# A residual block on one core: squares moved from GpSimd to ScalarE, two more plain input tiles, another first pair, a later forget gate

## The chip, the cores and the metric

The kernel runs on one core of a Trainium2 chip. The metric is the device time of one execution in microseconds (us), here the median of three runs. TensorE multiplies matrices, VectorE and ScalarE do elementwise work, GpSimd a little of it and some transfers, and SyncE's queue issues the other transfers.

## What is computed

One layer of a residual block on 528 tokens (16 learned ones and 512 of the input) of 2048 channels, in float32:

```python
h  = rmsnorm(r, mix_pre_g)
z  = h @ w_in + b_in          # q | k | v | forget logits | pool input | gates
logf = log_sigmoid(f_logit)   # 8 heads; its running sum over tokens biases the attention
attn = forgetting_attention(q, k, v, logf)
m  = sigmoid(g_attn) * (attn @ w_attn_o) + sigmoid(g_pool) * (pool(u) @ w_pool_o)
r  = r + rmsnorm(m @ w_out, mix_post_g)
r  = r + rmsnorm(conv_ffn(rmsnorm(r, ffn_pre_g)), ffn_post_g)
```

The change lies in the first part, `h @ w_in`, where q, k, v, the gates and the forget logits are made.

## The kernel before, in words

Channels lie on partitions, tokens along the row, so x is 16 tiles of 128 x 528 (`xr[k]`). A float32 product is made of three reduced ones: each operand is split into a high part, a ScalarE copy, and a low part, a VectorE subtraction; high times high, high times low and low times high are added up in a PSUM bank. For weights that is `make_hi` and `make_lo` (L193 and L201, tiles `whi` and `wlo`), for x `split_x` (L369 and L370, tiles `xb`, or `xh` and `xl` from k = 8 on), for token sums `split_sums` (L520 and L524, tiles `ht` and `lt`). The weights of 128 output channels, a tile, come in two halves of 1024 columns, each a "unit" with a high and a low part; six raw halves, four high and four low ones have a place.

The loop over k streams x. For every k it splits x, squares it (L396, L400, L402: ScalarE for even k and for 0 and 1, GpSimd for odd k) and adds the square up (`square_sum`, L382: even k on VectorE into one accumulator, odd k on GpSimd into another), and TensorE does 4 products for the forget logits (bank pair `pf`, L407) and 6 for the first tile of q (`pq`, L375). A product takes 264 columns, half of the tokens.

After that, tiles are made in one of two ways. A **plain tile** (`x_step`, banks `pk`) takes 16 x 6 = 96 products. A **pair** of tiles (`strassen`) takes 7 x 24 = 168 products, for two tiles, by a Strassen scheme with seven block products: its seven weight blocks are called 11, 12, S2, S1, S3, S4 and 22 (S1 to S4 are sums of blocks, made on VectorE, `wsum`), and they meet the blocks 11, 21, T2, T1, T3, 22 and T4 of x. T1 to T4 are the token sums: differences of token halves of x, made in place in `xr` by `sums_of_x` (L538 scales on ScalarE, L543 subtracts on VectorE), then split into `ht` and `lt`. Before, four tiles are plain (`NC = 4`) and the rest of q, k and v goes in ten pairs, then pool inputs and gates in further pairs.

The order of the work on each engine is the order in which the program records it. Two lanes of side work (`Side`) give out a piece at each step of TensorE's loops; a `yield` says how many microseconds of products should pass before the next piece. `norm_x` makes `rstd`, the factor of the norm, by a product with ones (`ps_rs`) and a reciprocal; `x_evac` (L589) multiplies the finished banks of a plain tile by `rstd` on VectorE, and `x_out` adds the bias on ScalarE (L578) and stores from GpSimd's queue. `logits` (L430, L431) empties `pf` after the second plain tile. `forget` computes log-sigmoid on 8 rows, by halves of 264 columns, and its running sum in ten doubling steps on VectorE (L435 to L459); it starts in the second lane with the first pair. In a pair, ScalarE's copy of bank `pua` (L491) has to be done before the third block product, which adds onto that bank.

Of the kernel before, what the change touches and what calls it, by code (L numbers as in the profile page):

```python
# [35 lines left out]
P = 128  # L36
# [38 lines left out]
def block(ctx, tc, xT, win, wf, wao, wpw, wpo, wout, wup, wdn, consts, out):  # L75
# [22 lines left out]

    order = []

    NC = 4
    qkv = [t for h in range(H) for t in (h, 8 + h, 16 + h)]
    xpairs = list(zip(qkv[NC::2], qkv[NC + 1::2]))
    gates = [(32 + i, 33 + i) for i in range(0, 32, 2)]
# [19 lines left out]
    }  # L124


    loads, units, base = [], [], []
    for key in order:
        base.append(len(units))
        if key[0] == "pair":  # L130
            at0 = len(loads)
            for src in key[1:]:
                loads += [(srcs[src[0]](src[1]), c) for c in (0, 1024)]
            units += [(i, at0) for i in ("11", "12", "S2", "S1", "S3", "S4", "22")]
        else:
# [32 lines left out]
    def make_source():  # L168
        i = at["sum"]
        kind, n = units[i]  # L170
        if kind == "":
            sources[i] = raw_of(n)
        else:
            a11, a12, a21, a22 = (raw_of(n + j) for j in range(4))
            if kind == "S2":
                for name in ("S1", "S2"):
                    sums[name] = wp.tile([P, 1024], F32, name="wsum", tag="wsum", bufs=2)
                dve.tensor_tensor(sums["S1"], a21, a22, op=OP.add)
                dve.tensor_tensor(sums["S2"], sums["S1"], a11, op=OP.subtract)  # L179
            elif kind == "S3":  # L180
                dve.tensor_tensor(a21, a11, a21, op=OP.subtract)
                drop(n)
            elif kind == "S4":
                dve.tensor_tensor(a12, a12, sums["S2"], op=OP.subtract)  # L184
            sources[i] = {"11": a11, "12": a12, "S3": a21, "S4": a12, "22": a22}.get(kind) or sums[kind]
        at["sum"] += 1

    def make_hi():
# [185 lines left out]
            for e in range(2):  # L374
                pe.matmul(pss[e], w[a], xb[e, k][b], start=k == 0 and j == 0, stop=k == KT - 1 and j == 2)  # L375

    xacc = [F("acc"), F("acc")]
    sq = {}

    def square_sum(k):  # L380
        if k >= 2:
            (pool if k % 2 else dve).tensor_tensor(xacc[k % 2], xacc[k % 2], sq.pop(k), op=OP.add)  # L382

    pf, pq = ([s_ps(n)[:, :XN] for _ in range(2)] for n in ("pf", "pq"))
    w_f = lambda k: wf_s2[k // 8][:, k % 8]
# [1 line left out]
    for k in range(KT):  # L387
        g = wfr[:, KT * H + k:KT * H + k + 1]
        if k == 0:
            split_f(0)  # L390
        split_x(k, g)
        if k == 1:
            w_q = weights("in", 0, ahead=0)
            split_f(1)
        if k < 2:
            act.activation(xacc[k], xr[k], AF.Square)  # L396
        else:
            sq[k] = F("sq")
            if k % 2:
                pool.tensor_tensor(sq[k], xr[k], xr[k], op=OP.mult)  # L400
            else:
                act.activation(sq[k], xr[k], AF.Square)  # L402
        if k >= 3:
            square_sum(k - 3)
        for j in range(2):
            for e in range(2):
                pe.matmul(pf[e], w_f(k), xb[e, k][j], start=k == 0 and j == 0, stop=k == KT - 1 and j == 1)  # L407
        for kk in ((), (0, 1))[k == 1] if k < 2 else (k,):
            x_step(pq, w_q(kk), kk)
        if k == 7:  # L410
            make_lo()
    for k in range(KT - 3, KT):
        square_sum(k)
    rstd = cp.tile([P, L], F32, name="rstd")
    c_dram = dp.tile([H, L], F32, name="c_dram")
# [2 lines left out]
    cmeta = cp.tile([2, H, META], F32, name="cmeta")  # L418

    def norm_x():  # L420
        dve.tensor_tensor(xacc[0], xacc[0], xacc[1], op=OP.add)
        yield 8.0
        rstd_from(xacc[:1], rstd, L)

    fx = F("fx")[:H]

# [6 lines left out]
    def forget():  # L433

        dve.tensor_tensor(fx, fx, rstd[:H], op=OP.mult)  # L435
        yield 2.0
        act.activation(fx, fx, AF.Identity, bias=cs[:H, C_BF:C_BF + 1])
        yield 2.0
        ab, ln = F("fab")[:H], F("fln")[:H]
        fa, fb = ab[:, :XN], ab[:, XN:]  # L440
        for e in range(2):
            x, fc = fx[:, XN * e:XN * (e + 1)], ln[:, XN * e:XN * (e + 1)]
            act.activation(fa, x, AF.Abs)
            act.activation(fa, fa, AF.Exp, scale=-1.0)
            yield 2.0
            dve.tensor_scalar(fb, fa, 1.0, None, op0=OP.add)
            yield 2.0
            act.activation(fc, fb, AF.Ln)
            yield 2.0
            dve.tensor_scalar(fb, fb, -1.0, None, op0=OP.add)  # L450
            dve.tensor_tensor(fa, fa, fb, op=OP.subtract)
            dve.tensor_tensor(fc, fc, fa, op=OP.add)
            dve.scalar_tensor_tensor(x, x, 0.0, fc, op0=OP.min, op1=OP.subtract)
            yield 2.0
        cur, nxt = fx, ab
        sh = 1
        while sh < L:
            dve.tensor_copy(nxt[:, :sh], cur[:, :sh])
            dve.tensor_tensor(nxt[:, sh:], cur[:, sh:], cur[:, :L - sh], op=OP.add)  # L459
            cur, nxt = nxt, (ln if nxt is ab else ab)  # L460
            sh *= 2
            yield 3.0
        nc.gpsimd.dma_start(c_dram, cur)
        nc.gpsimd.dma_start(cmeta, c_dram[:, :META].unsqueeze(0).to_broadcast([2, H, META]))
        yield 1.0
# [13 lines left out]
    def strassen(keys, blocks, n, skip=0, late=None):  # L479
# [26 lines left out]
        dve.tensor_tensor(gr, gr, c[:, skip:], op=OP.add)  # L506
        return zg, zv


    xts = {}  # L510
    qkv_dram = dp.tile([24, P, L], F32, name="qkv_dram")
# [20 lines left out]

    def sums_of_x():

        for k in range(HK + 1):
            if k < HK:
                for i in (k, HK + k):
                    act.activation(xr[i], xr[i], AF.Identity, scale=wfr[:, KT * H + i:KT * H + i + 1])  # L538
            yield 1.2
            if k < HK:  # L540
                (b11, b12), (b21, b22) = ((xr[i][:, :XN], xr[i][:, XN:]) for i in (k, HK + k))
                for dst, a, b in ((b11, b12, b11), (b12, b22, b12), (b22, b22, b11), (b21, b21, b22)):
                    dve.tensor_tensor(dst, a, b, op=OP.subtract)  # L543
            if 1 <= k <= KX:
                yield from split_sums(xts, x_tiles(k - 1), XN)
# [55 lines left out]
    XBLOCKS.update({n: lambda k, n=n: xts[n, k] for n in ("T1", "T2", "T3", "T4")})  # L601
    side.add(norm_x())
    side2.add(sums_of_x())
    for m in qkv[1:NC]:
        w = weights("in", m)
        pss = [s_ps("pk")[:, :XN] for _ in range(2)]
        for k in range(KT):
            x_step(pss, w(k), k)
            for lane in (side, side2):
                lane.tick(6 * XN / 2330.0)  # L610
        if m == qkv[1]:
            side.finish()
            logits()
            x_evac(qkv[0], pq)
        x_evac(m, pss)
    side2.finish()
    side2.add(split_sums(xts, [t for k in range(KX, HK) for t in x_tiles(k)], XN))
    side2.finish()
    side2.add(forget())
    for ma, mb in xpairs:  # L620
        last = (ma, mb) == xpairs[-1]
        za, zb = strassen((("in", ma), ("in", mb)), XBLOCKS, XN, late=d_loads() if last else None)
        side.add(x_out((ma, za), (mb, zb)))
    side.finish()
    side2.finish()

# [588 lines left out]
```

## Time and profile before

| | |
|---|---|
| median of 3 runs | 2671.09 us (2663.85 to 2672.19) |
| profiled execution | 2668.45 us |
| its span in the trace | 2666.6 us |
| TensorE busy | 2558.5 us, 96% |
| VectorE busy | 1937.9 us, 73% |
| ScalarE busy | 1210.7 us, 45% |
| GpSimd busy | 227.2 us, 9% |

Read the stretches of the span first: TensorE's busy time in each, and the granted clock beside it. Then the waits of TensorE name what it waited for, and the timeline of one engine shows in which order its instructions ran and how long each took. A row of a timeline that ends in x4 is four instructions that follow each other; its time runs from the start of the first to the end of the last. Where a row ends in brackets, the engine was idle before it, and the releaser is named.

### The profile page before, as it was taken

To read this page: it belongs to the slowest core of one execution; us is meant where nothing else is said; L and a number is where in the kernel's file an instruction comes from. 1 tells how busy PE (TensorE), PEld (TensorE's weight loads), DVE (VectorE), ACT (ScalarE), POOL (GpSimd) and SP (SyncE) were. 2 spreads that over 40 slices of the span, in tenths; PEclk is the share of its full clock that TensorE was granted. 3 is DMA by queue.
4 is the path that set the end of the run, shared out by engine and by line. 5 is a ranking of instruction groups with operands and counts; after the bars stand their busy time and mean duration, and the time that the engine had idled before them with its cause. 6 is when DMAs were issued, how large, how long until landed. Compare 5 with 4: busy or idle time off the path is not lost.

```text
span 2666.6 us, 46374 instructions
## 1 busy us (share of the span) xinstructions
PE 2558.5 (96%) x18949; PEld 2450.8 (92%) x18949; DVE 1937.9 (73%) x2542; ACT 1210.7 (45%) x1851; POOL 227.2 (9%) x369
## 2 busy tenths in 40 slices
PE   8899999999888999999899999999999999999995
PEld 7899999999878899999899999999999978888885
DVE  8887778778766653489798888888888844545456
ACT  5544444444544423455555555455555542222232
POOL 3000000000122210034000000000000000000003
PEclk9999999999998999999999999999999999999997
DMA  4333433343543453578753333333333343333323
GB/s 165 104 121 135 139 125 122 134 143 121 200 141 113 137 179 99 181 243 274 225 182 125 110 115 124 119 107 123 127 108 119 125 155 113 122 116 122 114 90 127
DMA packets 129269, 369.57 MB, mean 139 GB/s; under 512 B 15758, under 2 KB 42128, under 8 KB 129056
## 3 DMA queue, kind: packets, MB, share of 16 engines
q1 hardware_dynamic: 112064, 310.48, 35.7%
q0 software_dynamic: 16992, 56.14, 5.7%
q8 instruction: 148, 2.42, 0.4%
q14 instruction: 65, 0.53, 0.1%
HBM read 319.34 MB, written 47.21 MB: 137 GB/s over the span
## 4 chain that ended last, share of the span: by engine, by line
PE 82%; DVE 7%; issue 6%; DMA 2%; ACT 2%; POOL 1%; SPq 0%; POOLq 0%; DVEq 0%; ACTq 0%
PE pua L303 28%; PE pd L303 18%; PE puc L303 14%; PE pub L303 7%; PE pw L303 6%; PE pu L303 4%; PE pao L303 3%; DVE wlo L201 1%; PE ppo L303 1%; PE pa L742 1%; DMA t<-h_dram 1%; ACT whi L193 1%; DVE xb L370 0%; DVE xr L543 0%; DVE lt L524 0%
## 5 line engine op out<-in xcount | busy, mean ns | idle before, releaser
L201 DVE TENSOR_TENSOR wlo<-wraw,whi 128x1024 fp32r<-128x1024 f32 x566 | 696.8, 1235 | 216.9 <-ACT whi L193 216.7
L193 ACT CAST whi<-wraw 128x1024 fp32r<-128x1024 f32 x566 | 594.3, 1051 | 517.6 <-DVE wraw L184 176.4
L303 PE MATMUL pua<-lt,whi 128*128 128x258 f32 (+1 forms) x1632 | 464.1, 284 | 0.0
L303 PE MATMUL pua<-h,whi 128*128 128x258 f32 x1520 | 371.0, 284 | 5.1 <-ACT z L491 5.1
L303 PE MATMUL pua<-h,wlo 128*128 128x258 f32 x1216 | 344.4, 283 | 0.0
L303 PEld LDWEIGHTS pua<-lt,whi 128*128 128x128 f32 x1632 | 309.9, 190 | 0.0
L303 PEld LDWEIGHTS pua<-h,whi 128*128 128x128 f32 x1520 | 267.4, 190 | 5.3 <-ACT z L491 5.3
L193 ACT CAST whi<-wsum 128x1024 fp32r<-128x1024 f32 x136 | 142.9, 1051 | 255.8 <-DVE wsum L179 251.7
L303 PE MATMUL pd<-fl,whi 128*128 128x512 f32 x640 | 252.1, 394 | 1.1 <-DVE fl L293 1.1
L303 PE MATMUL pd<-fh,wlo 128*128 128x512 f32 x640 | 251.7, 393 | 0.0
L303 PE MATMUL pd<-fh,whi 128*128 128x512 f32 x640 | 251.2, 393 | 0.0
L303 PEld LDWEIGHTS pua<-h,wlo 128*128 128x128 f32 x1216 | 231.4, 190 | 0.0
L1072 DVE TENSOR_TENSOR yacc<-yacc,pd 128x512 f32<-128x512 f32 x144 | 98.8, 686 | 167.6 <-PE pd L303 167.5
L303 PE MATMUL pua<-ht,whi 128*128 128x264 f32 x720 | 206.0, 286 | 12.2 <-ACT z L491 10.1
L303 PE MATMUL pua<-ht,wlo 128*128 128x264 f32 x720 | 205.2, 285 | 0.0
L201 DVE TENSOR_TENSOR wlo<-wsum,whi 128x1024 fp32r<-128x1024 f32 x136 | 166.0, 1222 | 53.9 <-ACT whi L193 53.9
L303 PE MATMUL puc<-h,whi 128*128 128x258 f32 x912 | 196.2, 282 | 0.0
L303 PE MATMUL puc<-h,wlo 128*128 128x258 f32 x608 | 171.4, 282 | 0.0
L303 PE MATMUL puc<-lt,whi 128*128 128x258 f32 (+1 forms) x544 | 153.9, 283 | 0.0
L303 PEld LDWEIGHTS puc<-h,whi 128*128 128x128 f32 x912 | 151.3, 189 | 0.0
L303 PEld LDWEIGHTS pua<-ht,whi 128*128 128x128 f32 x720 | 136.4, 189 | 12.8 <-ACT z L491 10.3
L303 PEld LDWEIGHTS pd<-fl,whi 128*128 128x128 f32 x640 | 120.1, 188 | 30.2 <-DVE fl L293 2.3
(326 smaller groups left out, 6305.4 us busy)
## 6 DMA issues: line engine op xcount, KB each, us to landing
wraw<-wup SPq DMA_DIRECT2D x200, 512.0 KB, 3.8
wraw<-win SPq DMA_DIRECT2D x128, 512.0 KB, 4.0
wraw<-wdn SPq DMA_DIRECT2D x88, 512.0 KB, 3.6
wraw<-wout SPq DMA_DIRECT2D x56, 512.0 KB, 4.4
act_dram<-cv POOLq DMA_DIRECT2D x44, 256.0 KB, 5.0
y<-act_dram SPq DMA_DIRECT2D x44, 256.0 KB, 4.9
sig_dram<-z POOLq DMA_DIRECT2D x32, 264.0 KB, 4.5
sg<-sig_dram POOLq DMA_DIRECT2D x32, 264.0 KB, 4.2
```

The lines of the kernel that those rows point to most:

```text
L193: act.copy(ready[i][0], sources[i])
L201: dve.tensor_tensor(lo, sources.pop(i), f32(ready[i][0]), op=OP.subtract)
L303: pe.matmul(po, a, b[:, xs], start=k == 0 and j == 0 and not more, stop=k == nk - 1 and j == 2, skip_group_check=more)
L742: pe.matmul(pa[:, q0:], u, w, start=n == 0 and j == 0, stop=n == 4 and j == 2)
L1072: dve.tensor_tensor(yacc[i], yacc[i], ps, op=OP.add)
```

## The change

Six tiles are plain in place of four, so that nine pairs of q, k and v are left. All squares of x are made on ScalarE and all their sums on VectorE, into one accumulator; the squares of odd k stay in the loop over k, those of even k come after it. The weights of the first two plain tiles are split earlier (`make_lo` at k = 7, 14 and 15). The forget logits are taken out of their banks before the plain tiles; q's and the next two tiles' banks are emptied after the third plain tile. The first pair has a function of its own, with four banks: its products with x's own blocks, 21, 11 and 22, come first, then the four with token sums, and the token sums that are not yet split are split beside it. The forget gate starts after the second pair, does both halves at once, and has longer pauses.

```diff
-    NC = 4
+    NC = 6
+    LATE = ("11", "12", "S2", "S1", "S3", "S4", "22")
+    EARLY = ("12", "11", "S4", "S2", "S1", "S3", "22")
...
-            units += [(i, at0) for i in ("11", "12", "S2", "S1", "S3", "S4", "22")]
+            first = key == ("pair", ("in", xpairs[0][0]), ("in", xpairs[0][1]))
+            units += [(i, at0) for i in (EARLY if first else LATE)]
...
-            if kind == "S2":
+            if kind in ("S2", "S4") and (n, "S2") not in sums:
...
-    xacc = [F("acc"), F("acc")]
+    xacc = F("acc")
+    def square(k):
+        sq[k] = F("sq") if k != 1 else xacc
+        act.activation(sq[k], xr[k], AF.Square)
+
     def square_sum(k):
-        if k >= 2:
-            (pool if k % 2 else dve).tensor_tensor(xacc[k % 2], xacc[k % 2], sq.pop(k), op=OP.add)
+        if k != 1:
+            dve.tensor_tensor(xacc, xacc, sq.pop(k), op=OP.add)
...
-        if k < 2:
-            act.activation(xacc[k], xr[k], AF.Square)
-        else:
-            sq[k] = F("sq")
-            if k % 2:
-                pool.tensor_tensor(sq[k], xr[k], xr[k], op=OP.mult)
-            else:
-                act.activation(sq[k], xr[k], AF.Square)
-        if k >= 3:
-            square_sum(k - 3)
+        if k % 2:
+            square(k)
+        if k >= 7 and k % 2:
+            square_sum(k - 6)
...
-        if k == 7:
+        if k in (7, 14, 15):
             make_lo()
-    for k in range(KT - 3, KT):
+    for n, k in enumerate(range(0, KT, 2)):
+        square(k)
+        if n < 3:
+            square_sum(KT - 5 + 2 * n)
+    for k in range(0, KT, 2):
         square_sum(k)
...
     def norm_x():
-        dve.tensor_tensor(xacc[0], xacc[0], xacc[1], op=OP.add)
-        yield 8.0
-        rstd_from(xacc[:1], rstd, L)
+        yield 16.0
+        rstd_from([xacc], rstd, L)
...
-        ab, ln = F("fab")[:H], F("fln")[:H]
-        fa, fb = ab[:, :XN], ab[:, XN:]
-        for e in range(2):
...
+        ab, fb, ln = F("fab")[:H], F("fb")[:H], F("fln")[:H]
+        act.activation(ab, fx, AF.Abs)
+        act.activation(ab, ab, AF.Exp, scale=-1.0)
+        yield 4.0
...
-            yield 3.0
+            yield 9.0
...
+    def strassen_early(keys, blocks, n):
+        unit = pair_weights(*keys)
+        a, b, c, d = (s_ps(x)[:, :n] for x in ("pua", "pub", "puc", "pud"))
+        zg, zv = F("z"), F("z")
...
+        product(0, b, "21")
+        product(1, a, "11")
+        act.copy(gl, a)
+        product(2, d, "22")
+        dve.tensor_tensor(gl, gl, b, op=OP.add)
+        product(3, a, "T2", True)
+        act.copy(gr, a)
+        product(4, c, "T1")
+        dve.tensor_tensor(gr, gr, d, op=OP.add)
+        product(5, a, "T3", True)
+        act.copy(vr, a)
+        dve.tensor_tensor(gr, gr, c, op=OP.add)
+        product(6, a, "T4", True)
+        act.copy(vl, a)
+        dve.tensor_tensor(vr, vr, c, op=OP.add)
+        return zg, zv
...
     def sums_of_x():
+        yield 12.0
...
+    logits()
+    waiting = [(qkv[0], pq)]
     for m in qkv[1:NC]:
...
-        if m == qkv[1]:
+        waiting.append((m, pss))
+        if m == qkv[2]:
             side.finish()
-            logits()
-            x_evac(qkv[0], pq)
-        x_evac(m, pss)
+        if m not in qkv[:2]:
+            while waiting:
+                x_evac(*waiting.pop(0))
...
-    side2.finish()
-    side2.add(forget())
     for ma, mb in xpairs:
...
-        za, zb = strassen((("in", ma), ("in", mb)), XBLOCKS, XN, late=d_loads() if last else None)
+        keys = ("in", ma), ("in", mb)
+        if (ma, mb) == xpairs[0]:
+            za, zb = strassen_early(keys, XBLOCKS, XN)
+            side2.finish()
+        else:
+            za, zb = strassen(keys, XBLOCKS, XN, late=d_loads() if last else None)
         side.add(x_out((ma, za), (mb, zb)))
+        if (ma, mb) == xpairs[1]:
+            side2.add(forget())
```

Line numbers of the change are three higher up to the loop over k and some thirty higher after it. What stands in a row on an engine changes in three places on which the prediction rests.

VectorE (DVE) before, from the first half of q's weights (`wlo`) through the splits of x (`xb`, `xl`) to the first tile's end; `acc` is the accumulator of squares:

```order
L201 TENSOR_TENSOR wlo<-wraw,whi 128x1024
L352 TENSOR_TENSOR wf_s<-wfr,wf_s 128x8x8
L370 SCALAR_TENSOR_TENSOR xb<-xr,wfr,xb 128x264 x8
L382 TENSOR_TENSOR acc<-acc,sq 128x528
L370 SCALAR_TENSOR_TENSOR xb<-xr,wfr,xb 128x264 x4
L382 TENSOR_TENSOR acc<-acc,sq 128x528
L201 TENSOR_TENSOR wlo<-wraw,whi 128x1024
L370 SCALAR_TENSOR_TENSOR xl<-xr,wfr,xh 128x528 x2
```

GpSimd's seven squares and seven additions run beside this list. The same place in the change, up to the additions behind the last split of x:

```order
L204 TENSOR_TENSOR wlo<-wraw,whi 128x1024
L355 TENSOR_TENSOR wf_s<-wfr,wf_s 128x8x8
L373 SCALAR_TENSOR_TENSOR xb<-xr,wfr,xb 128x264 x12
L204 TENSOR_TENSOR wlo<-wraw,whi 128x1024
L373 SCALAR_TENSOR_TENSOR xl<-xr,wfr,xh 128x528 x2
L389 TENSOR_TENSOR acc<-acc,sq 128x528
...
L373 SCALAR_TENSOR_TENSOR xl<-xr,wfr,xh 128x528
L389 TENSOR_TENSOR acc<-acc,sq 128x528
L204 TENSOR_TENSOR wlo<-wraw,whi 128x1024
L389 TENSOR_TENSOR acc<-acc,sq 128x528 x11
```

The twelve `xb` now follow each other, four additions stay between the `xl`, and eleven stand behind everything that q needs; GpSimd has no instruction here.

VectorE before, from the evacuation of the last plain tile into the first pair (`wlo<-wsum` are the low parts of S2 and S1, `fx` is the forget gate):

```order
L589 TENSOR_TENSOR z<-pk,rstd 128x264 x2
L524 TENSOR_TENSOR lt<-xr,ht 128x528 x6
L201 TENSOR_TENSOR wlo<-wsum,whi 128x1024 x2
L181 TENSOR_TENSOR wraw<-wraw 128x1024
L435 TENSOR_TENSOR fx<-fx,rstd 8x528
```

All six `lt` stand ahead of S2's low part, which the third block product takes. In the change, from the last plain tile's evacuation on:

```order
L620 TENSOR_TENSOR z<-pk,rstd 128x264 x2
L204 TENSOR_TENSOR wlo<-wraw,whi 128x1024
L204 TENSOR_TENSOR wlo<-wsum,whi 128x1024
L554 TENSOR_TENSOR lt<-xr,ht 128x528 x2
L204 TENSOR_TENSOR wlo<-wsum,whi 128x1024
L184 TENSOR_TENSOR wraw<-wraw 128x1024
L554 TENSOR_TENSOR lt<-xr,ht 128x528 x4
```

The low parts of S4 and S2 now come ahead of the `lt`, and no forget step stands here.

ScalarE (ACT) before, in the first pair up to the copy of the first block product out of `pua`:

```order
L520 CAST ht<-xr 128x528 x6
L193 CAST whi<-wsum 128x1024
L578 ACTIVATE z<-z,cs 128x528
L437 ACTIVATE fx<-fx,cs 8x528
L491 COPY z<-pua 128x264
```

The copy stands behind a forget step. In the change:

```order
L550 CAST ht<-xr 128x528 x6
L609 ACTIVATE z<-z,cs 128x528
L196 CAST whi<-wsum 128x1024
L524 COPY z<-pua 128x264
L196 CAST whi<-wraw 128x1024 x2
```

The copy of `pua` now follows the high part of S1 and no forget step.

## Rows read from the trace of the kernel before

**Rows 1.** The page, busy time, share of the span and instructions of each engine.

```profile
PE 2558.5 (96%) x18949; PEld 2450.8 (92%) x18949; DVE 1937.9 (73%) x2542; ACT 1210.7 (45%) x1851; POOL 227.2 (9%) x369
```

**Rows 2.** Stretches: length, each engine's busy us, granted clock, DMA share, GB/s.

```profile
0.00:41.17 41.17, 28.27 (x159) 24.81 (x160) 35.10 (x39) 23.24 (x42) 20.29 (x21) 0.92 0.60 215
41.17:77.34 36.17, 36.17 (x294) 35.86 (x293) 32.84 (x58) 24.97 (x38) 1.82 (x3) 1.00 0.31 103
77.34:110.86 33.52, 22.96 (x171) 22.54 (x170) 25.61 (x35) 19.84 (x29) 0.54 (x1) 0.85 0.24 80
94.30:98.21 3.91, 3.91 (x18) 3.91 (x19) 2.36 (x2) 3.46 (x5) 0.00 (x0) 0.50 0.43 133
110.86:132.87 22.01, 20.75 (x170) 20.54 (x169) 20.28 (x32) 9.89 (x15) 1.08 (x2) 1.00 0.36 121
132.87:153.36 20.49, 20.49 (x170) 20.49 (x169) 18.55 (x28) 10.38 (x15) 1.62 (x4) 1.00 0.39 130
```

**Rows 3.** TensorE's waits from 75 to 140: total us, times, longest.

```profile
PE pua L303 <- ACT z L491: 10.1, 1, 10.1
PE pua L303 <- ACT z L496: 1.3, 1, 1.3
```

**Rows 4.** Timeline of VectorE, 0 to 45: start, us, instruction, count, idle before.

```profile
6.17 0.90 DVE L370 SCALAR_TENSOR_TENSOR xb<-xr,wfr,xb 128x264 fp32r<-128x264 f32 x2 [0.44 <-ACT xb L369]
11.21 9.78 DVE L370 SCALAR_TENSOR_TENSOR xb<-xr,wfr,xb 128x264 fp32r<-128x264 f32 x8
22.67 5.42 DVE L370 SCALAR_TENSOR_TENSOR xb<-xr,wfr,xb 128x264 fp32r<-128x264 f32 x4
28.01 1.81 DVE L382 TENSOR_TENSOR acc<-acc,sq 128x528 f32<-128x528 f32 x1
30.88 1.44 DVE L370 SCALAR_TENSOR_TENSOR xl<-xr,wfr,xh 128x528 fp32r<-128x528 f32 x2
32.24 0.70 DVE L382 TENSOR_TENSOR acc<-acc,sq 128x528 f32<-128x528 f32 x1
39.53 3.49 DVE L201 TENSOR_TENSOR wlo<-wraw,whi 128x1024 fp32r<-128x1024 f32 x3
```

**Rows 5.** Timeline of GpSimd, the first square and the last additions.

```profile
10.14 1.07 POOL L400 TENSOR_TENSOR sq<-xr 128x528 f32<-128x528 f32 x1 [7.87 <-DMA xr<-xT]
...
26.30 2.96 POOL L382 TENSOR_TENSOR acc<-acc,sq 128x528 f32<-128x528 f32 x2
```

**Rows 6.** Timeline of TensorE, third tile of x.

```profile
12.24 1.14 PE L407 MATMUL pf<-xb,wf_s 128*128 128x264 f32 x4
...
13.22 0.65 PE L375 MATMUL pq<-xb,whi 128*128 128x264 f32 x4
```

**Rows 7.** Timeline of ScalarE, 0 to 30.

```profile
10.95 1.72 ACT L369 ACTIVATE xb<-xr,wfr 128x264 fp32r<-128x264 f32 x4
...
14.73 0.63 ACT L402 ACTIVATE sq<-xr 128x528 f32<-128x528 f32 x1
...
16.08 1.04 ACT L193 CAST whi<-wraw 128x1024 fp32r<-128x1024 f32 x1
...
23.55 0.72 ACT L369 ACTIVATE xh<-xr,wfr 128x528 fp32r<-128x528 f32 x1
```

**Rows 8.** Timeline of VectorE and ScalarE in the first pair, 83 to 95.

```profile
85.26 3.80 DVE L524 TENSOR_TENSOR lt<-xr,ht 128x528 fp32r<-128x528 f32 x6 [1.01 <-ACT ht L520]
...
92.39 0.69 DVE L435 TENSOR_TENSOR fx<-fx,rstd 8x528 f32<-8x528 f32 x1
...
93.11 0.73 ACT L437 ACTIVATE fx<-fx,cs 8x528 f32<-8x528 f32 x1 [3.63 <-DVE fx L435]
93.87 0.38 ACT L491 COPY z<-pua 128x264 f32<-128x264 f32 x1
```

**Rows 9.** Timeline of VectorE, the reciprocal of the norm.

```profile
54.20 3.45 DVE L324 RECIPROCAL rstd<-rs_s 128x528 f32<-128x528 f32 x1 [2.05 <-ACT rs_s L323]
```

**Rows 10.** The page's DMA issues: count, KB each, us to landing.

```profile
sig_dram<-z POOLq DMA_DIRECT2D x32, 264.0 KB, 4.5
```

More of the change, by code (lines that the diff above doesn't have):

```diff
@@ L174, in make_source @@
             a11, a12, a21, a22 = (raw_of(n + j) for j in range(4))
-            if kind == "S2":
+            if kind in ("S2", "S4") and (n, "S2") not in sums:
                 for name in ("S1", "S2"):
[L177 to L180, printed above, removed]
+                    sums[n, name] = wp.tile([P, 1024], F32, name="wsum", tag="wsum", bufs=2)
+                dve.tensor_tensor(sums[n, "S1"], a21, a22, op=OP.add)
+                dve.tensor_tensor(sums[n, "S2"], sums[n, "S1"], a11, op=OP.subtract)
+            if kind == "S3":
                 dve.tensor_tensor(a21, a11, a21, op=OP.subtract)
@@ L183, in make_source @@
             elif kind == "S4":
-                dve.tensor_tensor(a12, a12, sums["S2"], op=OP.subtract)
-            sources[i] = {"11": a11, "12": a12, "S3": a21, "S4": a12, "22": a22}.get(kind) or sums[kind]
+                dve.tensor_tensor(a12, a12, sums[n, "S2"], op=OP.subtract)
+            sources[i] = {"11": a11, "12": a12, "S3": a21, "S4": a12, "22": a22}.get(kind) or sums[n, kind]
         at["sum"] += 1
@@ L438, in forget @@
         yield 2.0
-        ab, ln = F("fab")[:H], F("fln")[:H]
-        fa, fb = ab[:, :XN], ab[:, XN:]
-        for e in range(2):
[L442 to L454, printed above, removed]
+        ab, fb, ln = F("fab")[:H], F("fb")[:H], F("fln")[:H]
+        act.activation(ab, fx, AF.Abs)
+        act.activation(ab, ab, AF.Exp, scale=-1.0)
+        yield 4.0
+        dve.tensor_scalar(fb, ab, 1.0, None, op0=OP.add)
+        yield 4.0
+        act.activation(ln, fb, AF.Ln)
+        yield 4.0
+        dve.tensor_scalar(fb, fb, -1.0, None, op0=OP.add)
+        dve.tensor_tensor(ab, ab, fb, op=OP.subtract)
+        yield 4.0
+        dve.tensor_tensor(ln, ln, ab, op=OP.add)
+        dve.scalar_tensor_tensor(fx, fx, 0.0, ln, op0=OP.min, op1=OP.subtract)
+        del fb
+        yield 4.0
         cur, nxt = fx, ab
@@ L507, in strassen, with product @@
         return zg, zv
+    def strassen_early(keys, blocks, n):
+        unit = pair_weights(*keys)
+        a, b, c, d = (s_ps(x)[:, :n] for x in ("pua", "pub", "puc", "pud"))
+        zg, zv = F("z"), F("z")
+        def product(i, ps, block, more=False):
+            mm3([(ps, slice(0, n))], HK, unit(i), blocks[block], more)
+        gl, gr, vl, vr = zg[:, :n], zg[:, n:2 * n], zv[:, :n], zv[:, n:2 * n]
+        product(0, b, "21")
[14 more added lines that the diff above has]
+        return zg, zv
     xts = {}
```

## The prediction, as it was made

> **What bounds the kernel now.** I read the engines' shares first: TensorE is busy for 96% of the span and VectorE for 73% [rows 1], so time can come only from the remaining holes of TensorE. The stretches tell where those near the change lie [rows 2]. A later pair (132.87 to 153.36) runs 168 products in 20.49 us, all busy, so one product of 264 columns costs 0.122 us at the full clock. Against that rate three stretches lose time. In the first 41.17 us, in which x arrives, TensorE ran 160 products (4 for the forget logits and 6 for q on each of 16 tiles): 19.5 us of work. The first pair takes 33.52 us, 13.0 more than a later one, and the second 22.01 us, 1.5 more. The three plain tiles between them lose nothing.
>
> The first stretch. VectorE's 128x264 instructions take 0.45 us each while GpSimd does nothing (0.90 for two at 6.17); from 11.21 on eight of them take 9.78 and then four take 5.42, 1.27 us each [rows 4]. GpSimd's squares and sums run from 10.14 to 29.26 [rows 5]. An addition takes 1.81 us inside that time (at 28.01) and 0.70 after it (32.24). So twelve instructions lose about 10 us, and TensorE follows VectorE. That x's own transfers slow VectorE speaks against the rows: the fast two at 6.17 ran while x was being loaded too.
>
> The first pair. Its third product adds onto a bank that ScalarE must copy out first, and TensorE waits 10.1 us for that copy [rows 3]. The timeline shows why it is late [rows 8]: VectorE does six lt splits from 85.26, then weights, and only at 92.39 the forget gate's first step; ScalarE's next forget step waits for that one and starts at 93.11; the copy stands behind it and starts at 93.87. After the hole TensorE is granted 0.50, its 1.2 GHz level, for 3.91 us [rows 2]; that is inside the 13.0.
>
> **The change, part by part.**
>
> *Squares.* GpSimd loses seven squares and seven additions; ScalarE gets the seven squares, VectorE the additions. Even tiles are squared, and most sums made, after the last x tile is split, so these stand behind what TensorE needs. TensorE has finished q on the first two tiles at about 12.2 and reaches the full rate near 13.2 [rows 6]. Fourteen tiles of 10 products are then 140 x 0.122 = 17.1 us, with 0.2 for the slow beginning: q ends at 29.5. The two feeders must be done sooner. VectorE from 10.2: 0.2 for the second forget-weight split, 12 x 0.45 + 8 x 0.72 for the splits, 2 x 1.16 for weights, 4 x 0.70 for the sums that stay in the loop = 16.5, so 26.7 [rows 4]. ScalarE from 9.1: 12 x 0.43 + 8 x 0.72 + 7 x 0.63 + 2 x 1.04 = 17.4, so 26.5 [rows 7]; x is there by then, since it began the last tile at 23.55 without a wait. Hence TensorE itself ends last, with some 3 us to spare: 41.2 to 29.5, **-11.7**. If VectorE stayed as slow as it is, this would be 0; with no wait at all it cannot pass -12.2.
>
> The seven extra additions are 7 x 0.70 = 4.9 us on VectorE. The eleven that come after the loop end at about 37.7 (from 30: 11 x 0.70); the logits' two additions and the next weight split follow, to 39.7, and the tile that starts at 41.2 needs that split. So I cost them at nothing; with that cover gone they cost up to 4.9. The Trainium skill (Perfetto Trace Analysis, Optimizing Scalar/DVE Operations) says that a saturated VectorE may be relieved by giving work to ScalarE or even GpSimd, which speaks against bringing additions back; by it the sum would be 4.9 smaller. The same place warns that the two share a read port, and the 1.81 against 0.70 above is that case here.
>
> *Two more plain tiles in place of one pair.* A plain tile is 96 products, 11.7 us; two are 23.4 against 20.5: **+2.9**. The stretch with five of them must be fed: the last weight split of each half is the test. After the sums' product (about 48.2) VectorE does the reciprocal, 3.45 us [rows 9], which begins at about 49.3, three small steps of 0.7, an lt and a weight split: 56.8, needed at 59.8. For the next split come three lt of 0.7, four subtractions and six evacuations of 0.45 and the split itself: 64.6, needed at 66.1 (two-input instructions of 528 and 264 columns as in rows 4). Margins of 1.5 to 3 us: cost 0, up to +5 if they are gone. The banks of the third plain tile are those of the sums' product, free at 48.5; those of the fourth are q's, emptied by 62, needed at 65.6.
>
> *First pair.* It starts with three products that need no token sums, 72 x 0.122 = 8.8 us of cover in place of 5.9; the forget gate is no longer between the chain's copy and its bank; only the lt of tiles 5 to 7 (six) remain to be made. After the last plain tile's end at 89 VectorE has two evacuations, three weight splits, one sum and six lt, 0.7 + 3.4 + 1.2 + 4.2 = 9.5, plus a microsecond of waits for ScalarE's casts: 99.5; the last lt is needed 8.8 + 2.6 after 89, at 100.4. The 13.0 goes, and I leave 0.5 for a brush with this: **-12.5**. The fourth bank and the different weight order add no instruction to TensorE; weights on SP's queue are all there since the tiles before, only the next pair's are issued in another order.
>
> *Forget gate.* It starts after the second pair, in whole rows, its scan steps 9 us apart instead of 3. The second pair's 1.3 us wait for a ScalarE copy [rows 3] and its small change go: **-1.5**. Its Exp and Ln table loads become two in place of four, all beside TensorE. Its two stores move past twelve more q, k, v stores on GpSimd's queue, and its reader stands far behind, at the pool product. One wait is new: with one more 128x528 buffer held, ScalarE's fourth copy of the third pair takes the buffer of an earlier output and waits for its store, 4.5 us from issue to landing [rows 10]. It issues some 11 us into the pair, the copy is needed at 17.6: 0, at most 2.
>
> Sum: -11.7 + 2.9 - 12.5 - 1.5 = **-22.8**. The profiled execution took 2668.45, so 2645.7; the median of the runs, 2671.09, lies 2.6 above it. I take the median's 2671.09 - 22.8 = **2648**.
>
> **Rivals.**
>
> *VectorE becomes the bound of the plain tiles* by the 4.9 us it gained. For it: it is busy 32.84 of the 36.17 us there now [rows 2]. Against: the margins above. 2648 + 4.9 = 2653.
>
> *The first pair still waits*, on lt or on a weight sum, for as long as now: 10.1 us given back, 2658. For it: six lt and three sums still stand in a row on VectorE; against: the forget steps are out of the row and the cover is longer.
>
> *The slow splits are not GpSimd's doing*, so that the change does not do what it says: the first term falls to 0, 2660. Against it are both rows cited, with the addition at 28.01 the plainest.
>
> *Slower.* The five plain tiles are fed so late that TensorE idles before each half, and its clock falls as after the hole of the first pair: 18 products in 3.91 us, 0.217 each [rows 2]. For 480 products the loss is 480 x 0.095 = 45.6 us: 2694. It decides from where VectorE misses its margins by several microseconds at each half. The stretch of three tiles shows the clock at 1.00 throughout. The Trainium skill (TensorE: Matmul & The Clock Gate, What's actually happening) says that the throttled state is the default and that activity releases it; by that rule this case needs real gaps, which I do not see.
>
> **How the numbers follow.** The forecast gets 0.67, the bound VectorE 0.12, the first pair 0.09, the sharing 0.05, the slow clock 0.03; 0.04 is left for several of these shortfalls together. The range goes from 2641 (the lowest run before, 2663.85, less 22.8) to 2660 (the third rival, and the second with 2 us for the buffer). A difference under 0.3%, 8 us, can't be told from none here. Faster by more needs a gain of 8, which all but the last two cases have: 0.93; within it 0.04; slower 0.03.
>
> **What would show it.** In the changed profile: VectorE's 128x264 splits at 0.45 us to the end of x; the first plain product after q near 29.5, not 41.17; no TensorE wait over 1 us in the plain tiles; the first pair near 21 us from about 89, the later ones 20.5; the second pair starting near 110, after the same eight tiles that are done at 132.87 now (four plain and two pairs). Splits above 1 us, a first pair over 25, or a granted clock under 0.9 between 30 and 110 would prove me wrong.

## The result, and the profile after

| | before | changed |
|---|---|---|
| median of the runs beside each other | 2669.0 us (4 runs) | 2644.82 us (2642.21 to 2646.53, 4 runs) |
| ratio | | 0.9908, 95% interval 0.9895 to 0.9921 |
| span of the profiled execution | 2666.6 us | 2644.7 us |
| start of the first plain tile after q | 41.29 us | 30.75 us |
| start of the first pair | 77.46 us | 90.04 us |
| the first eight tiles, q among them, are done | 132.87 us | 111.22 us |
| first product of the pools, behind all pairs of q, k and v | 710.2 us | 689.1 us |

The time fell by 24.2 us; 2648 had been forecast, from a fall of 22.8. At the point where eight tiles are done the trace of the change is 21.65 us ahead, at the pools 21.1, at the end of the span 21.9. So the gain is made in the first 111 us, and in these two traces what follows changes it by no more than half a microsecond. The medians differ by 1.4 us more than forecast and the traces by 0.9 less; the interval of the ratio, 21 to 28 us, holds both.

Two of the marks, TensorE's timeline before and in the change. Its first product in the pair is at 77.46 (the stretch of [rows 2] begins with the last plain product, at 77.34), and the change begins its second pair at 111.22:

```profile
77.46 0.41 PE L303 MATMUL pua<-xb,whi 128*128 128x264 f32 x2
```

```profile
111.22 0.40 PE L306 MATMUL pua<-xb,whi 128*128 128x264 f32 x2
```

The page of the changed kernel, busy time, share and instructions, to be set beside [rows 1]:

```profile
PE 2553.9 (97%) x18973; PEld 2448.8 (93%) x18973; DVE 1919.1 (73%) x2537; ACT 1206.6 (46%) x1844; POOL 207.4 (8%) x355
```

TensorE does 24 more products, as the two plain tiles for a pair ask, and is busy 4.6 us less: products take less time each in the stretch of x (28.27 us for 159 [rows 2], 22.40 for 150 below) and in the first pair. GpSimd has the 14 instructions less that were taken from it.

The stretches of the changed kernel (columns as in [rows 2]):

```profile
0.00:29.50 29.50, 22.40 (x150) 21.64 (x151) 21.25 (x37) 24.57 (x46) 1.59 (x7) 1.00 0.87 318
29.50:88.00 58.50, 58.50 (x480) 58.37 (x479) 51.76 (x84) 32.65 (x48) 2.90 (x5) 1.00 0.33 105
88.00:110.00 22.00, 21.53 (x177) 21.32 (x176) 17.44 (x22) 12.46 (x18) 0.54 (x1) 1.00 0.31 109
110.00:132.00 22.00, 22.00 (x183) 22.00 (x182) 15.40 (x16) 10.56 (x15) 1.08 (x2) 1.00 0.35 121
132.00:153.00 21.00, 20.97 (x173) 20.75 (x172) 15.32 (x17) 13.80 (x20) 1.08 (x2) 1.00 0.40 126
```

From 29.5 to 153 TensorE is busy all but 0.5 us of 123.5, at 1.00 of its clock. (The first row reads 1.00 too, although its early products take 0.22 us each, as long as at the half rate; there the products' own times tell the rate, and they are shown further down.) The stretch of the first pair, 33.52 us with a clock of 0.85 before, has nothing left in it but that half microsecond. Transfers ran at 215 GB/s over the first 41 us before, and run at 318 over the first 29.5 now.

TensorE's waits in the changed kernel, from 0 to 160 (total, times, longest):

```profile
PE pf L408 <- ACT xb L372: 4.6, 1, 4.6
PE pq L378 <- ACT whi L196: 2.5, 1, 2.5
PE pua L306 <- ACT z L532: 0.5, 1, 0.5
```

The first two are the start, x's first tile and the first weight half, whose loads the change does not touch. The 10.1 us of [rows 3] are gone, and its 1.3 too.

VectorE's timeline in the changed kernel, to be set beside [rows 4] and [rows 9]:

```profile
10.74 1.70 DVE L373 SCALAR_TENSOR_TENSOR xb<-xr,wfr,xb 128x264 fp32r<-128x264 f32 x4
12.72 1.71 DVE L373 SCALAR_TENSOR_TENSOR xb<-xr,wfr,xb 128x264 fp32r<-128x264 f32 x4 [0.28 <-ACT xb L372]
...
26.46 0.76 DVE L373 SCALAR_TENSOR_TENSOR xl<-xr,wfr,xh 128x528 fp32r<-128x528 f32 x1
...
31.60 6.39 DVE L389 TENSOR_TENSOR acc<-acc,sq 128x528 f32<-128x528 f32 x8 [0.52 <-ACT fx L434]
...
50.51 3.45 DVE L327 RECIPROCAL rstd<-rs_s 128x528 f32<-128x528 f32 x1 [0.71 <-ACT rs_s L326]
...
56.72 1.22 DVE L204 TENSOR_TENSOR wlo<-wraw,whi 128x1024 fp32r<-128x1024 f32 x1
...
98.19 2.56 DVE L554 TENSOR_TENSOR lt<-xr,ht 128x528 fp32r<-128x528 f32 x4
```

Four splits of x take 1.70 us together, 0.43 each, where four took 5.42 before, and VectorE now even waits for ScalarE between them. The last split of x ends at 27.2 (forecast 26.7), the late sums end at 38.0 (37.7), the first weight split after the reciprocal ends at 57.9 (56.8), and the last lt of the first pair ends at 100.75 (99.5, with the pair itself starting a microsecond later than forecast).

### The profile page after: what moved, and what is told of

The parts are those of the page before. It is cut to its first block, busy times and chain, and to the rows that moved or that the text cites. A ratio compares the mean times of both kernels' runs of the same rounds, so it can differ in the third digit from the quotient of the medians.

```text
span 2644.7 us, 46390 instructions
## 1 busy us (share of the span) xinstructions
PE 2553.9 (97%) x18973; PEld 2448.8 (93%) x18973; DVE 1919.1 (73%) x2537; ACT 1206.6 (46%) x1844; POOL 207.4 (8%) x355
## 4 chain that ended last, share of the span: by engine, by line
PE 82%; issue 6%; DVE 6%; DMA 3%; ACT 1%; POOL 1%; SPq 0%; POOLq 0%; DVEq 0%; ACTq 0%
PE pua L306 27%; PE pd L306 18%; PE puc L306 13%; PE pub L306 7%; PE pw L306 6%; PE pao L306 3%; PE pu L306 2%; PE pk L378 2%; DVE wlo L204 1%; PE ppo L306 1%; PE pa L781 1%; DMA t<-h_dram 1%; PE pq L378 1%; ACT whi L196 1%; POOL mix L967 0%
## 5 line engine op out<-in xcount | busy, mean ns | idle before, releaser
L306 PE MATMUL pua<-lt,whi 128*128 128x258 f32 (+1 forms) x1608 | 455.9, 283 | 0.0
L306 PEld LDWEIGHTS pua<-lt,whi 128*128 128x128 f32 x1608 | 303.6, 189 | 0.0
L306 PE MATMUL pua<-ht,whi 128*128 128x264 f32 x696 | 198.3, 285 | 2.2 <-ACT z L499 1.7
L306 PE MATMUL pua<-ht,wlo 128*128 128x264 f32 x696 | 197.6, 284 | 0.0
L306 PEld LDWEIGHTS pd<-fh,whi 128*128 128x128 f32 x640 | 120.1, 188 | 28.4 <-ACT fh L295 0.5
```

Of the source, the lines that this page charges most:

```text
L306: pe.matmul(po, a, b[:, xs], start=k == 0 and j == 0 and not more, stop=k == nk - 1 and j == 2, skip_group_check=more)
```

## The experiments

The changed kernel ran once more, and nine variants of it or of the kernel before. The table gives each one's median, its ratio to the kernel before on the same chip with the 95% interval, and two marks from its profile: the start of the first plain tile, which ends the stretch of x, and the first product of the pools.

| run | median us | ratio | first plain tile | pools |
|---|---|---|---|---|
| before | 2669.0 | 1 | 41.29 | 710.2 |
| the change | 2644.82 | 0.9908 (0.9895 to 0.9921) | 30.75 | 689.1 |
| c1, the change again | 2645.94 | 0.9916 (0.9900 to 0.9933) | 31.15 | 689.2 |
| e1, GpSimd reads | 2661.19 | 0.9975 (0.9965 to 0.9985) | 41.99 | 701.3 |
| e2, GpSimd only writes | 2646.96 | 0.9921 (0.9906 to 0.9935) | 30.41 | 688.0 |
| e3, squares alone | 2660.47 | 0.9974 (0.9962 to 0.9986) | 30.86 | 704.8 |
| e4, four plain tiles | 2657.08 | 0.9958 (0.9943 to 0.9973) | 29.28 | 699.4 |
| e5, old first pair | 2648.63 | 0.9923 (0.9906 to 0.9940) | 30.52 | 689.1 |
| e6, early gate | 2650.80 | 0.9929 (0.9914 to 0.9943) | 29.41 | 689.8 |
| e7, seven more sums | 2649.43 | 0.9922 (0.9907 to 0.9937) | 30.08 | 690.4 |
| e8, old pair and early gate | 2649.13 | 0.9933 (0.9919 to 0.9948) | 30.24 | 691.6 |
| e9, six plain tiles alone | 2667.84 | 1.0001 (0.9992 to 1.0011) | 41.37 | 706.4 |

**c1: the same kernel again.** It is there to show how far a difference can be trusted.

> The changed kernel itself once more, beside the next two on one chip, to see by how much a second execution differs. Every theory: 2645 within 3 us, the first plain tile near 30.5, the second pair near 111.

Median 1.1 us from the first, the pools' mark 0.1 us from it, the first plain tile 0.4, all as expected. A variant that stands within 0.7 us of the change at the pools can still end 4 to 6 us later (e5, e6). No edit lies behind that mark, and from it to the end of the span the profiled executions take between 1955.3 us (e8) and 1959.6 (e6), the kernel before 1956.4. So up to some 4 us between two times need not come from what was edited. One trace of each does not tell whether they belong to the kernel or to the execution; the marks of the first 700 us are free of them.

### Is it GpSimd's reading that slows VectorE?

**e1** puts 14 GpSimd instructions with inputs in SBUF back into the loop over x; nobody reads what they write.

```diff
+        if k % 2 and k > 2:
+            t = F("gs")
+            pool.tensor_tensor(t, xr[k], xr[k], op=OP.mult)
+            pool.tensor_tensor(t, t, xr[k], op=OP.add)
```

> The changed kernel with 14 GpSimd instructions of two inputs (128x528) beside the loop over x, whose results nobody reads. Theory, GpSimd's reads slow VectorE's two-input instructions: the 128x264 splits rise from 0.43 to about 1.2 us, the first plain tile starts at 39 to 41 in place of 30.8, the time rises by 8 to 10 us to about 2654. Rival, the splits were slow because of what they waited for or because of x's transfers: 0.43, 30.8 and 2645 stay.

**e2** has GpSimd write as long a time, and read nothing.

```diff
+        if k % 2 and k > 2:
+            t = F("gs")
+            for _ in range(5):
+                pool.memset(t, 0.0)
```

> The same, but GpSimd only fills scratch tiles with zeros, 35 instructions of about 0.5 us, so busy for as long and reading nothing. Theory, it is GpSimd's reading that VectorE pays for: nothing changes, first plain tile at 30.8, 2645. Rival, any GpSimd instruction slows VectorE: splits near 1.2 us, first plain tile near 39, 2654. The Trainium skill (SBUF - State Buffer, Who interferes with whom) says the former of two-input VectorE instructions; no run so far shows it here.

Groups of VectorE and GpSimd in e1, 0 to 45 (busy us, mean ns of one, idle before):

```profile
L373 DVE SCALAR_TENSOR_TENSOR xb<-xr,wfr,xb 128x264 fp32r<-128x264 f32 x16 | 17.9, 1188 | 1.7 <-ACT xb L372 1.7
...
L407 POOL TENSOR_TENSOR gs<-gs,xr 128x528 f32<-128x528 f32 x7 | 10.4, 1492 | 0.5
L406 POOL TENSOR_TENSOR gs<-xr 128x528 f32<-128x528 f32 x7 | 8.6, 1230 | 8.5 <-DMA xr<-xT 8.5
```

The same groups in e2:

```profile
L373 DVE SCALAR_TENSOR_TENSOR xb<-xr,wfr,xb 128x264 fp32r<-128x264 f32 x16 | 6.8, 489 | 2.3 <-ACT xb L372 2.3
...
L407 POOL MEMSET gs<- 128x528 f32 x35 | 18.5, 538 | 1.6
```

And VectorE's in the change:

```profile
L373 DVE SCALAR_TENSOR_TENSOR xb<-xr,wfr,xb 128x264 fp32r<-128x264 f32 x16 | 6.8, 489 | 2.0 <-ACT xb L372 2.0
```

GpSimd is busy 19.0 us in the one and 18.5 in the other. Beside reading instructions a split takes 1188 ns, beside writing ones 489, which is its mean in the change without either. So it is neither GpSimd's being busy nor its writing; what e1 has and e2 has not is inputs in SBUF. (The two also differ in the kind of instruction, and one with a single input was not run.) The theory held in both runs, and both rivals fall. The Trainium skill (SBUF — State Buffer, Who interferes with whom) says that a VectorE instruction with two inputs in SBUF contends with a GpSimd instruction that reads SBUF and not with one that only writes; 1188 against 489 ns agrees.

The price was larger than the theory's 8 to 10 us: at the start of the first plain tile 41.99 less 30.75 is 11.2 us, the whole first term of the change and a little more, and the median lies 14.2 us above that of e2 on the same chip. TensorE was held up in tile after tile and then slowed by its clock as well, as the stretch from 16 to 30 in e1 shows:

```profile
16.00:30.00 14.00, 9.73 (x49) 8.29 (x49) 14.00 (x11) 12.76 (x21) 13.61 (x11) 0.79 0.65 252
```

VectorE is busy for all of it with 11 instructions, and TensorE, granted 0.79, does 49 products where the full rate would be 115 (14.00 / 0.122).

### What are the squares worth without the rest?

**e3** is the kernel before with the squares and their sums moved: four plain tiles, the norm still 8 us after the loop, the logits still taken out after the second plain tile. Its diff is the part of the change's diff from `xacc` to `rstd_from`, without the `yield`; the earlier weight splits at k = 14 and 15 are in it.

> The kernel before with the squares and their sums alone as in the change (four plain tiles, old first pair, early forget gate). Theory, the parts add up: first plain tile at about 31, the first pair still some 33 us long, so 10 us less than before, 2659. Rival, the gain is given back, since seven more additions on VectorE push its work for the first pair back: less than 5 us gained, the first pair's wait above 14 us.

TensorE's waits in e3, 0 to 160 (names and lines as in the kernel before):

```profile
PE pua L303 <- ACT z L492: 9.9, 1, 9.9
...
PE pk L375 <- DVE rs_a L322: 4.4, 1, 4.4
```

The first plain tile starts at 30.86, 10.4 us early as in the change; at the pools only 5.4 are left, by the medians about 7. That lies between the theory's 10 and the rival's under 5, and the second wait is why. VectorE's timeline in e3 around it, and TensorE's at its place:

```profile
32.14 6.40 DVE L386 TENSOR_TENSOR acc<-acc,sq 128x528 f32<-128x528 f32 x8 [0.51 <-DVE acc L386]
...
47.41 0.77 DVE L322 TENSOR_SCALAR rs_a<-ps_rs 128x264 f32<-128x264 f32 x2
```

```profile
47.98 0.92 PE L375 MATMUL pk<-xb,whi 128*128 128x264 f32 x4 [4.38 <-DVE rs_a L322]
```

The second plain tile needs the bank of the norm's product. VectorE comes to read that bank only at 47.41, behind the eight late sums, two weight splits, two lt and twelve token sums. In the whole change the norm's product is made later (`yield 16.0`), the token sums begin later (`yield 12.0`) and the logits leave their banks first, and no tile waits there. The prediction gave these edits no price of their own. Set beside e3, they keep about 5 us of the first term; no run takes them out one by one, so which of them is needed stays open.

### What took the hole out of the first pair?

**e4** is the change with four plain tiles.

```diff
-    NC = 6
+    NC = 4
```

> The change with four plain tiles in place of six, all else as in the change. Theory, the two extra plain tiles are cover for the norm's factor and the token sums, which VectorE finishes near 81: the first pair, now starting near 67, waits about 10 us, and 2.9 us of products are saved: 2652. Rival, the plain tiles only cost products: 2642.

TensorE's waits in e4, 0 to 160:

```profile
PE pud L306 <- DVE wlo L204: 9.5, 1, 9.5
...
PE pud L306 <- ACT whi L196: 1.8, 1, 1.8
```

VectorE's timeline in e4, up to the split that ends the wait, and TensorE behind it:

```profile
75.40 0.43 DVE L574 TENSOR_TENSOR xr<-xr 128x264 f32<-128x264 f32 x1 [1.19 <-ACT xr L569]
...
79.23 3.72 DVE L574 TENSOR_TENSOR xr<-xr 128x264 f32<-128x264 f32 x8
82.87 1.22 DVE L204 TENSOR_TENSOR wlo<-wraw,whi 128x1024 fp32r<-128x1024 f32 x1
```

```profile
84.14 0.59 PE L306 MATMUL pud<-xh,wlo 128*128 128x264 f32 x1 [9.47 <-DVE wlo L204]
```

The pair starts at 65.22, and for the next 17 us VectorE is still making token sums, their lt parts and the pair's weight sums, with the low half of the third block's weights queued behind them, at 82.87. After the wait TensorE is granted 0.57 for 3.91 us. Eight tiles are done at 121.53, 10.3 us later than in the change, and the median is 12.3 above it (10.1 above e2 on the same chip). The theory's wait came, and the time was 5 us worse than its 2652; the rival, that the plain tiles only cost products, falls. The whole first pair in e4, to the first product of the next:

```profile
65.22:101.07 35.85, 23.25 (x170) 22.22 (x169) 32.51 (x48) 19.03 (x28) 1.08 (x2) 0.86 0.24 77
```

So with the new order of products and the late gate, but four plain tiles, the first pair is no shorter than before (33.40 us, from 77.46 to 110.86). Two plain tiles cost 2.9 us of products and buy VectorE 23 us in which to finish the sums.

**e9** is the other side: the kernel before with six plain tiles and nothing else (`NC = 6`).

> The kernel before with six plain tiles in place of four and nothing else changed. Theory, the hole comes from the forget steps and the lt in one row, not from the number of tiles: the first pair still waits 8 to 10 us and 2.9 us of products are added, 2671. Rival, the two tiles alone give VectorE the time it lacks: the wait falls to under 4 us, 2663.

The wait of TensorE in e9's first pair, and VectorE's timeline just ahead of it; the pair begins at 100.96:

```profile
PE pua L303 <- ACT z L491: 3.8, 1, 3.8
```

```profile
101.03 0.77 DVE L589 TENSOR_TENSOR z<-pk,rstd 128x264 f32<-128x264 f32 x2 [6.26 <-PE pk L375]
101.72 3.79 DVE L524 TENSOR_TENSOR lt<-xr,ht 128x528 fp32r<-128x528 f32 x6
```

The hole of 10.1 us is 3.8 here, as the rival said and against the theory. VectorE has finished its other work early enough to wait 6.26 us for the last plain tile. Eight tiles are done at 127.84, 5.0 us ahead of before in these two profiles, and the pools' mark is 3.8 ahead; the medians show no difference, 0.9992 to 1.0011, between the theory's 2671 and the rival's 2663. So by itself this edit is worth nothing that the times show, and still most of the hole goes with it.

**e8** keeps the change's squares and six plain tiles, and puts back the old first pair together with the gate beside it.

```diff
-            units += [(i, at0) for i in (EARLY if first else LATE)]
+            units += [(i, at0) for i in LATE]
...
-            yield 9.0
+            yield 3.0
...
-            za, zb = strassen_early(keys, XBLOCKS, XN)
             side2.finish()
+            side2.add(forget())
+            za, zb = strassen(keys, XBLOCKS, XN)
...
-        if (ma, mb) == xpairs[1]:
-            side2.add(forget())
```

> The change with both the old first pair and the forget gate started with it (pauses of 3 us; both halves at once): six plain tiles and the new squares stay. Theory, the hole of 10.1 us is made by the forget steps ahead of the bank copy on ScalarE, behind six lt on VectorE: 6 to 10 us of waits come back in the first pair, 2653. Rival, the two extra plain tiles already took the hole away, since VectorE has the token sums done before the first pair starts: waits under 4 us, 2648.

The first pair in e8, three timelines: VectorE, ScalarE, TensorE.

```profile
90.30 3.80 DVE L554 TENSOR_TENSOR lt<-xr,ht 128x528 fp32r<-128x528 f32 x6
94.01 2.35 DVE L204 TENSOR_TENSOR wlo<-wsum,whi 128x1024 fp32r<-128x1024 f32 x2
...
97.41 0.69 DVE L439 TENSOR_TENSOR fx<-fx,rstd 8x528 f32<-8x528 f32 x1
```

```profile
98.14 0.73 ACT L441 ACTIVATE fx<-fx,cs 8x528 f32<-8x528 f32 x1 [5.68 <-DVE fx L439]
98.90 0.38 ACT L494 COPY z<-pua 128x264 f32<-128x264 f32 x1
```

```profile
99.33 0.59 PE L306 MATMUL pua<-ht,whi 128*128 128x264 f32 x1 [3.78 <-ACT z L494]
```

It is the chain of [rows 8], with the same six lt of 3.80 us, the same gate step, the same copy; from the first lt to the start of the copy it takes 8.6 us in both. But here the pair starts at 89.53 and the six lt at 90.30, 0.8 us into it; before, they began at 85.26 in a pair that started at 77.46, 7.8 us into it. VectorE's timeline before shows why: token sums, a weight split and two weight sums kept it until then, and it took up the last plain tile only at 83.48.

```profile
76.32 3.72 DVE L543 TENSOR_TENSOR xr<-xr 128x264 f32<-128x264 f32 x8
...
83.48 0.77 DVE L589 TENSOR_TENSOR z<-pk,rstd 128x264 f32<-128x264 f32 x2
```

Those 7.0 us of lateness make 10.1 out of 3.8, less 0.7 by which TensorE itself came later to its wait before. The theory, that the old pair and gate bring back most of the hole, fell; its rival, that they bring back less than 4, held.

**e5** puts back the old first pair but leaves the gate late (the first and third pieces of e8's diff, without `side2.add`). **e6** keeps the new pair and starts the gate with it, with its old pauses.

```diff
-            yield 9.0
+            yield 3.0
...
+    side2.add(forget())
...
             za, zb = strassen_early(keys, XBLOCKS, XN)
-            side2.finish()
...
-        if (ma, mb) == xpairs[1]:
-            side2.add(forget())
```

> The change with the first pair as it was: weights in the order 11, 12, S2, S1, S3, S4, 22, products with token sums from the third on, and the last six token tiles split ahead of it. Theory, with the forget gate gone from ScalarE's queue little is left of the 10.1 us: S2's low part is ready some 1 to 3 us late, 2647. Rival, the three free products are what removed the wait: 7 to 10 us come back, 2653.

> The change with the forget gate started with the first pair and with its old pauses of 3 us between scan steps (both halves at once, as in the change). Theory, its steps stand ahead of bank copies on ScalarE and of weights on VectorE: 2 to 4 us of waits in the first two pairs, 2648. Rival, its place does not matter once the first pair begins with free products: 2645, no wait over 1 us.

TensorE's waits in the first pairs of e5 and of e6 (one row of each):

```profile
PE pua L306 <- ACT z L499: 1.1, 1, 1.1
```

```profile
PE pua L306 <- ACT z L528: 2.2, 1, 2.2
```

Either edit alone leaves 1.1 or 2.2 us of the 3.8, both together 0.5. Both theories have the size of the waits, 1 to 3 us for e5 and 2 to 4 us for e6, and both rivals fall as to the waits; but in e5 the wait is for a ScalarE copy and not for S2's low part. The first pair, from its first product to that of the next, takes 33.40 us before, 26.88 in e9, 25.84 in e8, 23.66 in e6, 21.78 in e5 and 21.18 in the change. At the pools e5 stands exactly where the change does and e6 0.7 behind, though it had begun the first plain tile 1.3 earlier. With six plain tiles and a late gate, the order of the first pair's products is worth less than a microsecond at that mark.

### Is VectorE close to being the bound of the plain tiles?

**e7** adds seven more additions of 128x528 on VectorE behind the eleven late ones; their results are not read.

```diff
+    for k in range(7):
+        t = F("gs")
+        dve.tensor_tensor(t, xr[2 * k], xr[2 * k + 1], op=OP.add)
```

> The change with seven more additions of 128x528 on VectorE behind the eleven that follow the loop over x; nobody reads them. Theory, VectorE has some 3 us to spare there: the 4.5 us make TensorE wait 1 to 2 us at the second plain tile and nothing later, 2646. Rival of the prediction, VectorE is the bound of the plain tiles: the whole 4.5 us show, 2649.5.

VectorE's timeline in e7, and TensorE's at its one new wait:

```profile
36.80 4.41 DVE L421 TENSOR_TENSOR gs<-xr 128x528 f32<-128x528 f32 x7
```

```profile
43.06 0.51 PE L378 MATMUL pk<-xb,wlo 128*128 128x264 f32 x2 [0.68 <-DVE wlo L204]
```

4.41 us of extra work in the very place of the seven moved additions cost 0.7 us of waiting, where the theory had 1 to 2. So VectorE has about 3.7 us to spare there even on top of what the change gave it, and the additions it took over cost nothing. The median, 2649.43, happens to be the rival's 2649.5, but the rival asks for the whole 4.5 us in the plain tiles, and 0.7 are there. At the pools e7 is 1.3 us behind the change. The rest of the 4.6 us between the medians is what e5 shows as well, which ran on the same chip, has no such additions, stands at the change's own mark and ends at 2648.63.

## Why the prediction was right, and where its working was not

**Squares: forecast -11.7, measured -10.5** (41.29 to 30.75). Splits, feeders and the order of the ends came out as worked out. The missing 1.2 us lie at the beginning. The first weight half came later, q began at 9.49 in place of 9.05, after a wait of 2.5 us, and so the third tile of x began at 12.67 in place of 12.24 [rows 6]: 0.4 us. And the prediction let TensorE reach its full rate at 13.2, as in that row. TensorE's timeline in the changed kernel:

```profile
12.67 1.08 PE L408 MATMUL pf<-xb,wf_s 128*128 128x264 f32 x4
13.55 1.08 PE L378 MATMUL pq<-xb,whi 128*128 128x264 f32 x4
...
14.87 0.69 PE L408 MATMUL pf<-xb,wf_s 128*128 128x264 f32 x4
15.40 0.65 PE L378 MATMUL pq<-xb,whi 128*128 128x264 f32 x4
```

At 13.55 a product still takes 0.22 us, the half rate; the 0.122 pace is there at 15.40. The 14 products from 12.67 to 15.40 took 2.73 us; at the full rate, with the 0.2 that the prediction allowed, they would have taken 1.9. That is the other 0.8. In e4 and e6 q began at 8.83 and 8.90, the full pace was there at 12.69 and 12.83, and the first plain tile starts at 29.28 and 29.41: the forecast's 29.5. But the moment of the full pace does not simply follow q's start. TensorE's timeline in e7, then in e8:

```profile
8.38 1.25 PE L378 MATMUL pq<-xb,whi 128*128 128x264 f32 x4 [1.24 <-ACT whi L196]
...
13.77 1.08 PE L408 MATMUL pf<-xb,wf_s 128*128 128x264 f32 x4
```

```profile
9.81 1.25 PE L378 MATMUL pq<-xb,whi 128*128 128x264 f32 x4 [2.73 <-ACT whi L196]
...
13.68 0.65 PE L378 MATMUL pq<-xb,whi 128*128 128x264 f32 x4
```

e7 began q 1.4 us before e8, and is still at the half rate when e8 is at the full one. So the term took from one trace a moment that lies at 12.7 in one run and after 15 in another; what sets it stays open.

**Seven additions at nothing: right**, by e7. The rival that VectorE becomes the bound falls with it. Of the page that the prediction set beside it (the Trainium skill, Perfetto Trace Analysis, Optimizing Scalar/DVE Operations) these runs bear out the warning of the shared read port and not the advice to give work to GpSimd: its reads cost 11.2 us (e1), the seven additions on VectorE no wait of TensorE in the plain tiles.

**Two plain tiles: forecast +2.9, measured +2.6** (five tiles in 59.29 us, 30.75 to 90.04, against three in 36.17, 41.29 to 77.46, less a pair's 20.5). The size is right and the account is not: the step was written down as a cost alone. e4 shows that without it 10.3 us come back at the point where eight tiles are done, because VectorE has not finished its token sums when the first pair starts.

**First pair: forecast -12.5, measured -12.2** (33.40 to 21.18). The step that failed is the reason: the prediction let the hole go by the longer cover and by the gate leaving the chain. e9 and e8 show the hole at 3.8 with the old pair and an early gate as soon as there are six plain tiles, so 6.3 of the 10.1 us went with those; 3.3 more went with the new order and the late gate, and 0.5 is left. And e4, which has the new order and the late gate without the two tiles, waits 9.5 us. The prediction had the row that told it, the six lt at 85.26 with the pair under way since 77.34 [rows 2, 8], and read in it what stood in the chain but not how late the chain began. That the size of the term came out is luck as far as its reason goes: the edits were made together, and the two tiles, booked as a cost, did the larger part.

**Forget gate: forecast -1.5, measured -1.6** for the pair behind the first (22.01 to 20.45, 111.22 to 131.67). The reason given, that the gate starts after that pair, is not what the runs show. In e8 the gate runs beside the second pair and TensorE does not wait in it; in e6 it waits 0.2 us, and in e9, with six plain tiles and the old gate by halves, 0.7 of the 1.3. What takes the rest away was not singled out. The new wait for a buffer in the third pair, 0 to 2 us, came out at 0: TensorE is busy 20.97 of 21.00 us there.

The terms add up to the mark where eight tiles are done: -10.5 + 2.6 - 12.2 - 1.5 = -21.6, the step from 132.87 to 111.22. (The -1.5 stands in it for the pair that is no longer among the eight: its 22.01 us, less the 20.5 already taken off with the plain tiles.) The other rivals: that the sharing is not GpSimd's doing falls by e1 and e2; that the first pair still waits falls by the 0.5 us above; the slow clock in the plain tiles falls by the 1.00 from 29.5 to 88. The clock did fall where a feeder was late: after waits of 9.5 us (e4), 4.4 (e3) and 3.8 (e8 and e9) the next 3.9 us were granted 0.57, 0.59, 0.63 and 0.50.

No variant that ran is faster than the change; e2, c1 and e5 are within 4 us of it, which a measurement here does not tell from none. What is left before 111 us is the 7.1 us of start and the half rate up to about 15; no run was made for that.

## What to carry to other kernels

Ask of a chain not only what stands in it but when its first link began, and what kept that engine busy until then: here two plain tiles ahead of the chain, in which that engine could finish, took more of the wait (6.3 us) than another order of the products and taking the gate out (3.3). A part of a change that costs time by its own count can be what the gains of the others rest on, and such parts do not add: six plain tiles alone gave nothing that the times show, and without them the change lost about half of its gain. Before a GpSimd instruction is given work to relieve VectorE, look at the length of VectorE's two-input instructions inside and outside its time.

## What the runs showed of the hardware

- GpSimd busy with writes for 18.5 us left VectorE's splits at 489 ns, as without it, while 19.0 us of reading instructions made them 1188 (e2, e1). The size of the loss for TensorE was not expected: it waits about 1.07 us in each of four tiles, and then its granted clock falls as well, to 0.79 over the stretch from 16 to 30.
- After one wait of 3.8 us the next 3.9 us were granted 0.63 in e8 and 0.50, the 1.2 GHz level, in e9. The price of a hole is more than its length, and not the same each time.
- Near its start TensorE's products took the half rate's 0.22 us each, and the full pace was there at 12.69 in e4, at 13.68 in e8 and in the change only between 14.87 and 15.40. The granted clock reads 1.00 over that whole beginning in the change (0 to 29.5), so it does not tell the rate there.
